# Feed-forward nets: hi and lo of x as one moving operand of 512 columns

## The chip, the cores and the metric

The kernel runs on one core of one Trainium2 chip. The metric is device time in microseconds (us) of one execution. The core has a matrix engine (TensorE, PE in the rows; its weight loads are shown as PEld), a vector engine (VectorE, DVE), an activation engine (ScalarE, ACT), a programmable engine (GpSimd, POOL) and a queue that issues transfers (SyncE, SP). Matrix products are written to PSUM, which here is used as eight banks of 128 x 512 float32. DVE and ACT read PSUM, GpSimd does not; SBUF is the memory that all engines share.

## The reference

x is 256 positions by 1024 channels. Four layers work on it, two of one kind of net and two of another, each a mixer (attention, a gated recurrence, or three attention branches) followed by a feed-forward net. The feed-forward nets are what the change touches:

```
def conv_ffn(h, w_in, conv_w, conv_b, w_out):            # nets 1 and 2, h = rms_norm(x)
    z = causal_dwconv(h @ w_in, conv_w, conv_b)          # w_in: 1024 x 5632
    u, g = jnp.split(z, 2, axis=-1)
    return (jax.nn.gelu(g) * u) @ w_out                  # w_out: 2816 x 1024

a = depthwise_conv(h @ w_ffn_gate, conv_w, conv_b)       # nets 3 and 4
x = x + (jax.nn.gelu(a) * (h @ w_ffn_up)) @ w_ffn_down
```

All is float32. The kernel keeps that precision with the faster float32r products: each operand is split into hi (rounded) and lo (the rest), and a product is hi*hi + hi*lo + lo*hi.

## The kernel before

All weights lie in DRAM as one stream of 240 chunks in the order of use. `_push` (L245) loads the next chunk of up to 128 x 2048 values on the SP queue into a tile st, ACT writes hi from it (L258) and DVE writes lo = st - hi (L259), each in two halves of 1024 columns. st, hi and lo have three buffers each, and `chunk` (L265) keeps two chunks ahead of the one in use.

`mm3` (L273 to L277) issues the three products of a split operand pair. In `tm_wide` (L289) the weights chunk is the moving operand, 512 columns at a time. In `fm_pair` (L299) and `fm_first` (L545) the weights chunk is what is loaded into the array and x, transposed (channels on partitions, 256 positions as columns), is the moving operand: for each block of 128 input channels k and each half e of the chunk there are a product of the hi weights with xh (L275), of the hi weights with xl (L276) and of the lo weights with xh (L277), each of 256 columns, all added up in the same 256 columns of a bank.

`norm` (L337) transposes x on PE into banks S and T and writes xh with ACT and xl with DVE, as two tiles. The factor 1/rms of each position is not put into xh and xl: `norm_rows` (L370) spreads it over the partitions as the tile rb, and `times_r` (L563) multiplies the finished products by it on DVE as it takes them out of PSUM (L568, L570).

`ffn` (L574) is one feed-forward net. It has 22 steps j. Each takes a chunk of 128 columns of u and 128 of g: `fm_first` does j = 0 and 1 in banks A, A and S, S, `fm` (L557) the others in one bank each, T and S in turn. Then `times_r`, the convolution `conv` (ACT at L537, then DVE per further tap at L540), gelu on ACT and the product with u on DVE (L604, L605 in nets 1 and 2, where u and g are both convolved; L615, L616 in nets 3 and 4, where g alone is), and `split` (ACT at L307, DVE at L308), which leaves hi and lo of the hidden block in hg tiles. From j = 5 on, after each odd j, one `tm_wide` multiplies the pair of blocks from two pairs earlier (LAG) with its rows of w_out into four banks A, A, A, O; the last two pairs follow after j = 21. Net 2 also runs `before_b` (L761) before its steps: positions, sines and other scalars of the next layers, with several tables loaded by ACT.

PSUM: one pool with tags A (3 banks), S (2), T (2), O (1). All tiles of one tag take its banks in turn, and a tile waits until the former one in its bank has been read.

The order within each engine's queue is set by the framework's planner, from the order in which the code names the instructions, their dependencies and its own costs; each engine then works through its queue in that order. An instruction that waits at the head of a queue holds up all that stands behind it. GpSimd has little to do before: some bias tables in attention (L863) and a few transfers.

Of the kernel before, what the change touches and what calls it, by code (L numbers as in the profile page):

```python
# [12 lines left out]
F32R = mybir.dt.float32r  # L13
I32 = mybir.dt.int32
AF = mybir.ActivationFunctionType
ALU = mybir.AluOpType
AX = mybir.AxisListType
PSUM = bass.MemoryType.PSUM

P = 128  # L20
S = 256
D = 1024
KD = D // P
# [174 lines left out]
class InOrder:  # L198


    def __init__(self, tc, engine):
        self.tc, self.engine = tc, engine
# [6 lines left out]
class Net:  # L209
    def __init__(self, ctx, tc, ap, out, shapes, vat, rat, upto=99):  # L210
        self.tc, self.nc, self.ap, self.out = tc, tc.nc, ap, out
        self.shapes, self.vat, self.rat, self.upto = shapes, vat, rat, upto
        self.sb = ctx.enter_context(tc.tile_pool(name="sb", bufs=1))
        self.ps = ctx.enter_context(tc.tile_pool(name="ps", bufs=1, space=PSUM))
        self.n = 0
        self.q, self.qpos, self.off = [], 0, 0
        self.ph = "s"
        self.vec_o, self.act_o = InOrder(tc, self.nc.vector), InOrder(tc, self.nc.scalar)
        self.pool_o, self.sync_o = InOrder(tc, self.nc.gpsimd), InOrder(tc, self.nc.sync)


    PS = {"A": 3, "S": 2, "T": 2, "O": 1}
    SB = {"st": 3, "hi": 3, "lo": 3, "o": 4, "hg": 8, "w6": 2, "w4": 6, "w2": 2, "qk": 2, "s": 4, "pT": 2, "bias": 2, "ty": 24, "at": 4}

    def t(self, shape, tag, dt=F32):
        self.n += 1
        pool = self.ps if tag in self.PS else self.sb
        return pool.tile(shape, dt, tag=tag, name=f"{tag}_{self.ph}_{self.n}", bufs=self.PS.get(tag) or self.SB.get(tag, 1))

    def bank(self, tag):  # L230
        return self.t([P, 512], tag)

    def wide_banks(self):
        return [[self.bank("A"), self.bank("A")], [self.bank("A"), self.bank("O")]]
# [97 lines left out]
    def update(self, t, n, banks):  # L332
        xs = self.x[:, t, n * 512:n * 512 + 512]
        if banks is not None:
            self.nc.vector.tensor_tensor(out=xs, in0=banks[t][n][:, :], in1=xs, op=ALU.add)

    def norm(self, gi, banks=None, update=None):  # L337


        nc = self.nc  # L340
        update = update or self.update
        xh = self.t([P, KD, S], "xh", F32R)
        xl = self.t([P, KD, S], "xl", F32R)
        ss = self.t([P, 2, 2], "ssx")
        for n in range(2):
            for t in range(2):
                update(t, n, banks)
            for kp in range(2):
                pt = self.bank("ST"[kp])
                for e in range(2):  # L350
                    k = 4 * n + 2 * kp + e
                    for t in range(2):
                        nc.tensor.transpose(pt[:, e * S + t * P:e * S + t * P + P], self.x[:, t, k * P:k * P + P], self.ident)
                for e in range(2):
                    k = 4 * n + 2 * kp + e
                    g = self.vec(f"gain{gi}", k)
                    z = pt[:, e * S:e * S + S]
                    nc.scalar.activation(xh[:, k, :], z, AF.Copy, scale=g)  # L358
                    nc.vector.scalar_tensor_tensor(xl[:, k, :], z, g, xh[:, k, :].bitcast(F32), op0=ALU.mult, op1=ALU.subtract)  # L359
        for n in range(2):  # L360
            for t in range(2):
                sq = self.t([P, 512], "w2")
                nc.scalar.activation(sq, self.x[:, t, n * 512:n * 512 + 512], AF.Square, scale=1.0 / 32, accum_out=ss[:, n, t:t + 1])
        m = self.t([P, 16], "ty")
        nc.vector.scalar_tensor_tensor(m[:, :2], ss[:, 0, :], EPS, ss[:, 1, :], op0=ALU.add, op1=ALU.add)
        self.r = self.t([P, 2], "r")
        self.rsqrt(m[:, :2], 2, self.r)
        return xh, xl

    def norm_rows(self):  # L370

        nc = self.nc
        dg = self.t([P, 2, P], "w2")
        pb = self.bank("T")
        for t in range(2):
            nc.scalar.activation(dg[:, t, :], self.ident, AF.Copy, scale=self.r[:, t:t + 1])
            nc.tensor.matmul(pb[:, t * P:t * P + P], self.ones, dg[:, t, :], start=True, stop=True)
        self.rb = self.t([P, S], "rb")
        nc.scalar.activation(self.rb, pb[:, :S], AF.Copy)
# [183 lines left out]
    def times_r(self, z, src):  # L563
# [7 lines left out]
                                    in1=self.rb[:, None, :].to_broadcast([P, 2, S]), op=ALU.mult)  # L571
        return z

    def ffn(self, gi, body, ahead=None):  # L574
        xh, xl = self.norm(gi, self.acc)
        first = self.fm_first(xh, xl)
        self.norm_rows()
        acc = None
        if ahead is not None:
            ahead()  # L580
        done = []
        for j in range(NF):
            if j % 2 == 0:
                hh, hl = self.t([P, 2, S], "hg", F32R), self.t([P, 2, S], "hg", F32R)
                done.append((hh, hl))
            z = self.times_r(self.t([P, 2, S], "s"), first[j] if j < 2 else self.fm(xh, xl, "TS"[j % 2]))
            m = body(j, z[:, 0, :], z[:, 1, :])
            self.split(hh[:, j % 2, :], hl[:, j % 2, :], m)
            if j % 2 and j > 2 * LAG:
                if acc is None:  # L590
                    acc = self.wide_banks()
                kk = j - 1 - 2 * LAG
                self.tm_wide(acc, *done[kk // 2], kk, False)
        for kk in range(NF - 2 * LAG, NF, 2):
            self.tm_wide(acc, *done[kk // 2], kk, kk == NF - 2)
        self.acc = acc

    def ffn_a(self, l, gi, ahead=None):
        nc = self.nc
# [512 lines left out]
    def hybrid(self, i, g0):  # L1112
        nc = self.nc
        xh, xl = self.norm(g0, self.acc, self.pending)
        if i:
            self.layer_scalars(i)
        c, kr, skr = self.mla_prep(i, xh, xl)
# [11 lines left out]
        for kind, b in MERGE:  # L1129
            if kind == "gate":  # L1130
                gates[b] = []
                for jp in range(4):
                    g = self.times_r(self.t([P, 2, S], "hg"), self.fm(xh, xl, "A")).rearrange("p e s -> p (e s)")
                    nc.scalar.activation(g, g, AF.Tanh, scale=0.5)
                    gates[b].append(g)
                continue
            if b == 2:
                mh, ml = self.t([P, KD, S], "xh", F32R), self.t([P, KD, S], "xl", F32R)
            for jp in range(4):
                if jp % 2 == 0:  # L1140
                    wh, wl = self.chunk(4, 512)
                bk = self.bank("A")
                self.fm_pair(bk, *outs[b], wh, wl, 4, (jp % 2) * 256)
                m = merged[jp // 2][:, jp % 2, :]
                g = gates[b][jp]
                if b == 0:
                    nc.vector.scalar_tensor_tensor(m, g, 1.0, bk, op0=ALU.add, op1=ALU.mult)
                else:
                    nc.vector.scalar_tensor_tensor(g, g, 1.0, bk, op0=ALU.add, op1=ALU.mult)
                    nc.vector.tensor_tensor(out=m, in0=m, in1=g, op=ALU.add)  # L1150
                if b == 2:
                    d = (slice(None), slice(2 * jp, 2 * jp + 2), slice(None))
                    m2 = m.rearrange("p (e s) -> p e s", e=2)
                    nc.scalar.activation(mh[d], m2, AF.Copy, scale=0.5)
                    nc.vector.scalar_tensor_tensor(ml[d], m2, 0.5, mh[d].bitcast(F32), op0=ALU.mult, op1=ALU.subtract)
# [12 lines left out]
        xh, xl = self.norm(g0 + 2, self.acc)  # L1168
# [4 lines left out]
        e = [self.t([P, D], "w4") for _ in range(2)]  # L1173
# [10 lines left out]
        for t in range(2):  # L1184
            for n in range(2):
                c = slice(n * 512, n * 512 + 512)
# [18 lines left out]
    def build(self):  # L1205
        nc = self.nc
        steps = [self.start, self.pool_attn, lambda: self.ffn_a(0, 1), lambda: self.rglru(2), lambda: self.ffn_a(1, 3, self.before_b),
                 lambda: self.hybrid(0, 4), lambda: self.hybrid(1, 7)]
        update = None
        for n, f in enumerate(steps[:self.upto + 1]):  # L1210
            self.ph = str(n)
            self.pending = update
            update = f()
        for n in range(2):
            for t in range(2):
                (update or self.update)(t, n, self.acc)
                c = slice(n * 512, n * 512 + 512)
                nc.sync.dma_start(self.out[t * P:t * P + P, c], self.x[:, t, c])


def _program(nc, tc, ap, out, shapes, vat, rat, upto=99):
# [14 lines left out]
```

## Time and profile before

| | |
|---|---|
| time, median of 3 runs (lowest to highest) | 1530.11 us (1529.07 to 1530.61) |
| time of the profiled execution | 1529.12 us |
| its span in the profile | 1527.4 us |
| busy PE, PEld | 1505.9 us (99%), 1354.4 us (89%) |
| busy DVE, ACT, POOL | 1136.1 us (74%), 940.3 us (62%), 53.7 us (4%) |
| instructions | 25319 |

The span goes from the first to the last instruction in the trace; 1.7 us of the execution lie around it. PE's records overlap each other (a product's record lasts longer than the distance to the next), so its busy share says only that it hardly ever paused; what a product costs is the distance from its start to the next one's start.

### The profile page before, as it was taken

To read this page: it belongs to the slowest core of one execution; us is meant where nothing else is said; L and a number is where in the kernel's file an instruction comes from. 1 tells how busy PE (TensorE), PEld (TensorE's weight loads), DVE (VectorE), ACT (ScalarE), POOL (GpSimd) and SP (SyncE) were. 2 spreads that over 40 slices of the span, in tenths; PEclk is the share of its full clock that TensorE was granted. 3 is DMA by queue.
4 is the path that set the end of the run, shared out by engine and by line. 5 is a ranking of instruction groups with operands and counts; after the bars stand their busy time and mean duration, and the time that the engine had idled before them with its cause. 6 is when DMAs were issued, how large, how long until landed. Compare 5 with 4: busy or idle time off the path is not lost.

```text
span 1527.4 us, 25319 instructions
## 1 busy us (share of the span) xinstructions
PE 1505.9 (99%) x10020; PEld 1354.4 (89%) x10020; DVE 1136.1 (74%) x2189; ACT 940.3 (62%) x1675; POOL 53.7 (4%) x45
## 2 busy tenths in 40 slices
PE   8999999999999999999999999999999999999998
PEld 6689999898999998898898999988888889999996
DVE  6559777789897777877677766678886767866666
ACT  6746555586675556676755655556777674654554
POOL 0200000000000000001110000000000110000000
PEclk9999999999999999999999999999999999999999
DMA  8445455434465554442444555444442435454551
GB/s 296 157 170 194 173 191 189 166 138 170 162 209 177 194 182 162 165 151 84 159 139 167 192 192 180 180 168 181 172 166 88 145 122 193 166 190 172 191 193 55
DMA packets 37878, 257.33 MB, mean 168 GB/s; under 512 B 4384, under 2 KB 4768, under 8 KB 8320
## 3 DMA queue, kind: packets, MB, share of 16 engines
q1 hardware_dynamic: 36864, 252.45, 46.2%
q0 software_dynamic: 896, 3.28, 0.6%
q8 instruction: 78, 1.28, 0.3%
q14 instruction: 40, 0.33, 0.1%
HBM read 254.66 MB, written 1.05 MB: 167 GB/s over the span
## 4 chain that ended last, share of the span: by engine, by line
PE 86%; DVE 7%; ACT 4%; issue 2%; DMA 0%; SPq 0%; ACTq 0%
PE A L276 13%; PE A L275 13%; PE A L277 13%; PE S L276 6%; PE S L277 6%; PE S L275 6%; PE T L277 6%; PE T L276 6%; PE T L275 5%; DVE lo L259 2%; PE O L275 2%; PE O L276 2%; PE O L277 2%; ACT hi L258 1%; PE T L817 1%
## 5 line engine op out<-in xcount | busy, mean ns | idle before, releaser
L259 DVE TENSOR_TENSOR lo<-st,hi 128x1024 fp32r<-128x1024 f32 (+2 forms) x480 | 572.0, 1208 | 163.6 <-ACT hi L258 160.7
L258 ACT ACTIVATE hi<-st 128x1024 fp32r<-128x1024 f32 (+2 forms) x480 | 489.0, 1042 | 243.5 <-PE T L276 110.0
L277 PE MATMUL S<-xh,lo 128*128 128x256 f32 x752 | 214.1, 285 | 0.0
L276 PE MATMUL S<-xl,hi 128*128 128x256 f32 x752 | 213.3, 284 | 0.0
L275 PE MATMUL S<-xh,hi 128*128 128x256 f32 x752 | 212.0, 282 | 0.0
L277 PE MATMUL T<-xh,lo 128*128 128x256 f32 x704 | 200.5, 285 | 0.0
L276 PE MATMUL T<-xl,hi 128*128 128x256 f32 x704 | 199.9, 284 | 0.0
L275 PE MATMUL T<-xh,hi 128*128 128x256 f32 x704 | 199.0, 283 | 0.0
L276 PE MATMUL A<-xl,hi 128*128 128x256 f32 x496 | 143.7, 290 | 1.2 <-DVE xl L359 1.1
L275 PE MATMUL A<-xh,hi 128*128 128x256 f32 x496 | 144.4, 292 | 0.0
L275 PEld LDWEIGHTS S<-xh,hi 128*128 128x128 f32 x752 | 142.7, 190 | 0.1
L277 PE MATMUL A<-xh,lo 128*128 128x256 f32 x496 | 142.3, 287 | 0.0
L277 PEld LDWEIGHTS S<-xh,lo 128*128 128x128 f32 x752 | 142.2, 189 | 0.1
L276 PEld LDWEIGHTS S<-xl,hi 128*128 128x128 f32 x752 | 141.7, 188 | 0.0
L275 PEld LDWEIGHTS T<-xh,hi 128*128 128x128 f32 x704 | 133.5, 190 | 1.6
L276 PEld LDWEIGHTS T<-xl,hi 128*128 128x128 f32 x704 | 132.6, 188 | 1.5
L277 PEld LDWEIGHTS T<-xh,lo 128*128 128x128 f32 x704 | 133.1, 189 | 0.1
L275 PE MATMUL A<-hi,xh 128*128 128x512 f32 (+2 forms) x336 | 129.4, 386 | 0.2 <-ACT xh L358 0.2
L276 PE MATMUL A<-lo,xh 128*128 128x512 f32 (+2 forms) x336 | 128.4, 383 | 0.3 <-DVE lo L259 0.3
L277 PE MATMUL A<-hi,xl 128*128 128x512 f32 (+2 forms) x336 | 127.9, 383 | 0.0
L276 PE MATMUL A<-lo,hg 128*128 128x512 f32 x294 | 116.2, 395 | 0.4 <-DVE lo L259 0.4
L275 PE MATMUL A<-hi,hg 128*128 128x512 f32 x294 | 116.2, 395 | 0.0
(343 smaller groups left out, 2966.1 us busy)
## 6 DMA issues: line engine op xcount, KB each, us to landing
st<-in_w_dram SPq DMA_DIRECT2D x230, 1024.0 KB, 4.8
st<-in_w_dram SPq DMA_DIRECT2D x4, 832.0 KB, 4.4
st<-in_w_dram SPq DMA_DIRECT2D x2, 768.0 KB, 5.1
x<-in_x_dram SPq DMA_DIRECT2D x2, 512.0 KB, 4.1
st<-in_w_dram SPq DMA_DIRECT2D x4, 256.0 KB, 6.7
st<-in_w_dram SPq DMA_DIRECT2D x2, 512.0 KB, 3.4
w<-in_gain_dram POOLq DMA_DIRECT2D x2, 512.0 KB, 3.6
out_dram<-x SPq DMA_DIRECT2D x4, 256.0 KB, 2.0
```

Source lines behind the costliest of these rows:

```text
L258: nc.scalar.activation(hi[:, c0:c1], st[:, c0:c1], AF.Copy)
L259: nc.vector.tensor_tensor(out=lo[:, c0:c1], in0=st[:, c0:c1], in1=hi[:, c0:c1].bitcast(F32), op=ALU.subtract)
L275: mm(out, ah, bh, start=start, stop=False)
L276: mm(out, ah, bl, start=False, stop=False)
L277: mm(out, al, bh, start=False, stop=stop)
L817: nc.tensor.transpose(pt[:, kb * S + t * P:kb * S + t * P + P], p[:, t * S + kb * P:t * S + kb * P + P], self.ident)
```

## The change

The feed-forward nets get xh and xl as one tile xx of 128 x 8 x 512: for each k, 256 columns of hi and behind them 256 of lo. The hi weights are multiplied with all 512 columns at once, and the lo weights with the first 256 (`mm2`). So the left half of a bank adds up hi*hi + lo*hi and the right half hi*lo, and a step needs two banks, one for each e. `join` adds the halves: ACT copies the right halves to SBUF (a tile y), DVE adds them to the left halves, and GpSimd multiplies the sum by rb. `times_r` is left to the other layers.

PSUM is now two pools: A and O as before, and a second half of four banks that is S, S, T, T outside of the feed-forward nets and D, D (two tiles of two banks) inside; it is closed and opened anew where a net begins and ends. In a net, `norm` and `norm_rows` take D tiles, `wide_first` does j = 0 and 1 in A, A, A, O, and `wide` does the others in D tiles. In the last mixer, the tiles mh and ml become halves of one xx tile.

```diff
-    PS = {"A": 3, "S": 2, "T": 2, "O": 1}
+    PS = {"A": 3, "S": 2, "T": 2, "O": 1, "D": 2}
...
+    def half_of_psum(self, name):
+        if self.ps2 is not None:
+            self.ps2_close()
+        cm = self.tc.tile_pool(name=f"ps_{name}_{self.n}", bufs=1, space=PSUM)
+        self.ps2 = cm.__enter__()
+        self.ps2_close = lambda: cm.__exit__(None, None, None)
+        self.doubles = name == "D"
...
-        xh = self.t([P, KD, S], "xh", F32R)
-        xl = self.t([P, KD, S], "xl", F32R)
+        self.xx = self.t([P, KD, 2 * S], "xx", F32R)
+        xh, xl = self.xx[:, :, :S], self.xx[:, :, S:]
...
+            both = self.t([P, 2, 512], "D") if self.doubles else None
...
-                pt = self.bank("ST"[kp])
+                pt = both[:, kp, :] if self.doubles else self.bank("ST"[kp])
...
+    def mm2(self, out, wh, wl, xx, start, stop):
+        mm = self.nc.tensor.matmul
+        mm(out, wh, xx, start=start, stop=False)
+        mm(out[:, :S], wl, xx[:, :S], start=False, stop=stop)
+
+    def wide_first(self):
+        xx = self.xx
+        w = [self.chunk(KD, 256) for _ in range(2)]
+        banks = self.wide_banks()
+        for k0 in (0, 4):
+            for j in range(2):
+                for e in range(2):
+                    for k in range(k0, k0 + 4):
+                        c = slice(e * P, e * P + P)
+                        self.mm2(banks[j][e], w[j][0][:, k, c], w[j][1][:, k, c], xx[:, k, :], k == 0, k == KD - 1)
+        return banks
+
+    def wide(self):
+        d = self.t([P, 2, 512], "D")
+        wh, wl = self.chunk(KD, 256)
+        for e in range(2):
+            for k in range(KD):
+                c = slice(e * P, e * P + P)
+                self.mm2(d[:, e, :], wh[:, k, c], wl[:, k, c], self.xx[:, k, :], k == 0, k == KD - 1)
+        return d
+
+    def join(self, z, src):
+        nc = self.nc
+        y = self.t([P, 2, S], "w2")
+        parts = [(z[:, e, :], y[:, e, :], src[e]) for e in range(2)] if isinstance(src, list) else [(z, y, src)]
+        for zz, yy, b in parts:
+            nc.scalar.activation(yy, b[..., S:], AF.Copy)
+            nc.vector.tensor_tensor(out=zz, in0=b[..., :S], in1=yy, op=ALU.add)
+        nc.gpsimd.tensor_tensor(out=z, in0=z, in1=self.rb[:, None, :].to_broadcast([P, 2, S]), op=ALU.mult)
+        return z
+
     def ffn(self, gi, body, ahead=None):
-        xh, xl = self.norm(gi, self.acc)
-        first = self.fm_first(xh, xl)
+        self.half_of_psum("D")
+        self.norm(gi, self.acc)
+        first = self.wide_first()
...
-            z = self.times_r(self.t([P, 2, S], "s"), first[j] if j < 2 else self.fm(xh, xl, "TS"[j % 2]))
+            z = self.join(self.t([P, 2, S], "s"), first[j] if j < 2 else self.wide())
...
         self.acc = acc
+        self.half_of_psum("ST")
```

## Rows read from the trace of the kernel before

**Rows 1.** From the page: busy time, and the chain that ended last.

```profile
PE 1505.9 (99%) x10020; PEld 1354.4 (89%) x10020; DVE 1136.1 (74%) x2189; ACT 940.3 (62%) x1675; POOL 53.7 (4%) x45
...
PE 86%; DVE 7%; ACT 4%; issue 2%; DMA 0%; SPq 0%; ACTq 0%
```

**Rows 2.** Busy time by stretch: length, PE, PEld, DVE, ACT, POOL, granted clock, DMA.

```profile
115.00:138.00 23.00, 23.00 (x196) 23.00 (x196) 22.51 (x44) 17.35 (x29) 0.00 (x0) 1.00 0.54 184
138.00:280.50 142.50, 142.50 (x987) 132.58 (x987) 110.17 (x170) 79.92 (x119) 0.00 (x0) 1.00 0.53 186
404.00:427.40 23.40, 23.40 (x197) 23.40 (x196) 23.36 (x78) 21.18 (x34) 3.59 (x2) 1.00 0.39 136
844.00:867.00 23.00, 23.00 (x194) 23.00 (x194) 20.83 (x34) 15.03 (x24) 0.00 (x0) 1.00 0.51 184
867.00:1009.00 142.00, 142.00 (x987) 132.39 (x986) 97.74 (x135) 72.64 (x101) 0.00 (x0) 1.00 0.52 186
```

**Rows 3.** Timeline of PE in net 1, start and length: first product per block.

```profile
194.88 0.28 PE L275 MATMUL T<-xh,hi 128*128 128x256 f32 x1
...
200.63 0.28 PE L275 MATMUL S<-xh,hi 128*128 128x256 f32 x1
...
206.40 0.40 PE L275 MATMUL A<-hi,hg 128*128 128x512 f32 x1
...
212.00 0.28 PE L275 MATMUL T<-xh,hi 128*128 128x256 f32 x1
```

**Rows 4.** Timeline of PE: four transposes of 128 columns to a row.

```profile
101.13 0.60 PE L353 MATMUL S<-ident,x 128*128 128x128 f32 x4
101.56 0.60 PE L353 MATMUL T<-ident,x 128*128 128x128 f32 x4
```

**Rows 5.** Groups by line: shapes, count, busy us and mean ns, idle before.

```profile
L570 DVE TENSOR_TENSOR s<-T,rb 128x512 f32<-128x512 f32 x43 | 29.7, 691 | 66.1 <-PE T L277 66.1
...
L819 ACT ACTIVATE pT<-T 128x512 f32<-128x512 f32 x40 | 23.6, 590 | 4.4 <-PE T L817 4.1
```

**Rows 6.** What DVE waited for from 138 to 280.5 us: total, times, longest.

```profile
DVE s L570 <- PE T L277: 15.7, 8, 2.0
DVE lo L259 <- ACT hi L258: 8.5, 16, 0.8
DVE hg L308 <- ACT hg L307: 3.9, 8, 0.5
DVE qk L605 <- ACT qk L604: 3.8, 7, 0.5
```

**Rows 7.** Two GpSimd operations, a cast beside them, and minimum, median, maximum of lines.

```profile
705.11 3.62 POOL L863 TENSOR_SCALAR bias<-dist 128x512 f32<-128x512 f32 x2 [294.55 <-DVE at L877]
...
706.16 1.22 DVE L259 TENSOR_TENSOR lo<-st,hi 128x1024 fp32r<-128x1024 f32 x1
...
L1039 DVE TENSOR_SCALAR ty<-at,neglam x8: 206/358/645, 708.0 to 1192.5; 128x2 f32<-128x2 f32 x8
...
L863 POOL TENSOR_SCALAR bias<-distw x16: 1479/1490/1793, 719.6 to 1237.1; 128x512 f32<-128x512 f32 x16
```

**Rows 8.** Timeline of PE, DVE and ACT around the first `tm_wide` of net 2.

```profile
415.88 0.28 PE L275 MATMUL T<-xh,hi 128*128 128x256 f32 x1
...
421.16 0.68 DVE L570 TENSOR_TENSOR s<-S,rb 128x512 f32<-128x512 f32 x1
...
425.61 1.05 ACT L258 ACTIVATE hi<-st 128x1024 fp32r<-128x1024 f32 x1
...
427.64 1.22 DVE L259 TENSOR_TENSOR lo<-st,hi 128x1024 fp32r<-128x1024 f32 x1
...
428.92 0.50 PE L276 MATMUL A<-lo,hg 128*128 128x512 f32 x1 [0.42 <-DVE lo L259]
```

**Rows 9.** Timeline of DVE and PE at the end of net 1.

```profile
282.91 0.42 DVE L308 TENSOR_TENSOR hg<-qk,hg 128x256 fp32r<-128x256 f32 x1
...
286.08 0.40 PE L275 MATMUL A<-hi,hg 128*128 128x512 f32 x1
```

More of the change, by code (lines that the diff above doesn't have):

```diff
@@ L214, in __init__ @@
         self.ps = ctx.enter_context(tc.tile_pool(name="ps", bufs=1, space=PSUM))
+        self.ps2, self.ps2_close = None, None
         self.n = 0
@@ L226, in t @@
         self.n += 1
-        pool = self.ps if tag in self.PS else self.sb
+        pool = self.sb if tag not in self.PS else self.ps if tag in "AO" else self.ps2
         return pool.tile(shape, dt, tag=tag, name=f"{tag}_{self.ph}_{self.n}", bufs=self.PS.get(tag) or self.SB.get(tag, 1))
@@ L373, in norm_rows @@
         dg = self.t([P, 2, P], "w2")
-        pb = self.bank("T")
+        pb = self.bank("D" if self.doubles else "T")
         for t in range(2):
@@ L1137, in hybrid @@
             if b == 2:
-                mh, ml = self.t([P, KD, S], "xh", F32R), self.t([P, KD, S], "xl", F32R)
+                mm = self.t([P, KD, 2 * S], "xx", F32R)
+                mh, ml = mm[:, :, :S], mm[:, :, S:]
             for jp in range(4):
@@ L1209, in build @@
         update = None
+        self.half_of_psum("ST")
         for n, f in enumerate(steps[:self.upto + 1]):
@@ L1218, in build @@
                 nc.sync.dma_start(self.out[t * P:t * P + P, c], self.x[:, t, c])
+        self.ps2_close()
 def _program(nc, tc, ap, out, shapes, vat, rat, upto=99):
```

## The prediction

> **What bounds the kernel now.** I read the page first: PE is busy 99% of the span, and 86% of the chain that ended last is PE [rows 1]. A busy share of overlapping records proves little, so the next view is busy time by stretch, over the four feed-forward nets: PE has no idle time in them, at a granted clock of 1.00, the 2.4 GHz level [rows 2]. In the steady part of nets 1 and 2 DVE is at 110.17 of 142.50 us (77%) and ACT at 79.92 (56%); in nets 3 and 4, which convolve g alone, DVE is at 97.74 of 142.00. But in the heads of the nets (j = 2 to 5, before the first `tm_wide`) DVE is at 22.51 of 23.00 us in net 1, 23.36 of 23.40 in net 2, where ACT is at 21.18 too, and 20.83 of 23.00 in net 3. So PE is the bound, and in two heads the others have nothing to spare.
>
> The timeline of PE gives the prices [rows 3]. The 48 products of a step take 200.63 - 194.88 = 5.75 us and the next 48 take 5.77, so 120 ns per 256 columns. The 24 products of a `tm_wide` take 212.00 - 206.40 = 5.60 us, 233.3 ns per 512 columns. A pair of steps with its `tm_wide` lasts 17.12 us.
>
> **What the change does, part by part.**
>
> *Products.* Per k and e, three of 256 columns (3 x 120 = 360 ns) become one of 512 and one of 256. Columns stay the same, 768; one issue and one weight load go. At the prices above the two cost 233.3 + 120 = 353.3 ns, 6.7 ns less. There are 4 nets x 22 steps x 2 halves x 8 k = 1408 of them: -9.4 us. This alternation is not in the trace. One bound: 512 columns cost as much as two times 256, gain 0; a loss I exclude, as nothing is streamed in addition. The other: a product beside a long one costs only what a 128-column transpose does, (101.56 - 101.13) / 4 = 108 ns [rows 4], so 341 ns and -26 us. I take -9.4, which uses prices of the same stretch. A pair of steps then lasts 32 x 0.3533 + 5.60 = 16.91 us.
>
> The Trainium skill (TensorE: Matmul & The Clock Gate, Back-to-back issue gap) gives a warm isolated product N/2.4 + 2.5 ns. An estimate from that page: 215.8 and 109.2 ns, so 2.5 ns saved per triple, 3.5 us in all. The rows, 233 and 120 ns, are longer than the rule, and the part that doesn't grow with the columns is larger in them, which speaks for the larger gain.
>
> *DVE.* The multiplication out of PSUM, 691 ns [rows 5], becomes an addition of the same shape with one operand from PSUM: 0.
>
> *ACT.* One copy of 128 x 512 out of PSUM per step; the nearest row is 590 ns [rows 5]. Per pair ACT goes from 79.92 / 142.5 x 17.12 = 9.6 to 10.8 of 16.9 us. It hides behind PE in the steady part.
>
> *GpSimd.* One product of 128 x 512 per step on an engine that does nothing else there. The trace has only one-input operations of that size: 1.49 us alone, and the two at 705.11 took 3.62 together, so one was stretched by 0.64 while a DVE cast ran [rows 7]. Between 1.49 us and twice that plus the stretch, 3.6; I take 2.2. It adds latency, not load. What it takes from DVE is between nothing (the cast at 706.16 ran beside it in 1.22 us, as did the one at 427.64 without [rows 8]) and 0.44 us (a small TENSOR_SCALAR, 645 ns against 206, [rows 7]); I take 0.2 per step. DVE per pair: 110.17 / 142.5 x 17.12 = 13.24, then 13.6 of 16.9. Its waits for ACT, 8.5 + 3.9 + 3.8 = 16.2 us in 8.3 pairs [rows 6], make 1.95 more: 15.6. It still fits, with 1.3 to spare; in nets 3 and 4 with far more.
>
> *Latency.* From the end of a step's products to hg, the way grows by copy, product and their hand-overs, about 0.6 + 2.2 + 0.2 = 3 us. Between steps the LAG of two pairs covers it. At the end of net 1 the last split starts at 282.91 and ends at 283.33, and `tm_wide` of that pair starts at 286.08 [rows 9]: a reserve of 2.75, so some 0.3 us late; 0.6 for nets 1 and 2. In 3 and 4 two taps less are on the way: 0.
>
> *Double banks.* A step may now be issued only when the step two before has been joined, where there were four banks of S and T. A D tile has one step (5.65 us) for its join in the heads, and one step and a `tm_wide` later. In net 2 the step that ends at 415.88 is taken out only from 421.16 to 421.84, 5.96 us later [rows 8]: this head is where depth runs out, and the copy comes on top.
>
> *Head of net 2.* ACT's queue holds the table loads of `before_b`, and the cast of the first `tm_wide` chunk (425.61, then DVE at 427.64) is already late: PE waits 0.42 us for it at 428.92 [rows 8]. Before that cast ACT gets copies of four steps, two of them in halves: about 5 x 0.6 = 3 us more in a stretch with 2.2 us idle, minus the 0.4 us by which PE itself comes earlier. I put the stall at +3.1 us (0 to 6). In net 1 ACT is at 17.35 of 23.00, DVE is full but gets only five times 0.2 us: 0.3.
>
> *Start of the nets.* The first product needs xl as well as xh, some 0.1 us per net. In return joining needn't wait for rb. 0.1 in all. The reopened pools wait for tiles that were read long before: 0. Weight stream, transfers and the other layers: unchanged, 0.
>
> *Sum.* -9.4 + 0.6 + 3.1 + 0.3 + 0.1 = -5.3 us, made against the profiled execution of 1529.12 us (span 1527.4 and 1.7 around it). This lies 1.0 us under the median of 1530.11; from the median, 1524.8. I predict 1525.
>
> **Rivals.** About 0.2%, 3.1 us, is what a measurement of this kernel can tell from no change.
>
> *The gain is used up at heads and tails.* The same gain, but the head of net 2 costs 5 us, that of net 1 one, and each of the four tails 0.5: -9.4 + 8 = -1.4, some 1529. For it: the head of net 2 is full on both engines, and the depth of banks there is short by the numbers of rows 8. Against it: 5 us is nearly two steps' reserve, and casts run two chunks ahead. A smaller gain of the product pair, as by the rule above, ends in the same place.
>
> *DVE becomes the bound in nets 1 and 2 (slower).* The queues work in a fixed order. If the convolution on ACT stands waiting for the GpSimd product, and DVE's taps behind it, the time that DVE stands still comes off its reserve. By rows 2, 3 and 6 the reserve is 16.91 - 13.24 - 1.95 = 1.7 us per pair, 0.85 per step: from there on it decides. At 1.49 us per step, the length of one GpSimd operation, a pair is 1.3 us too long: 9 pairs x 2 nets = 23 us, and the two heads, which have no reserve, some 5 steps x 1.0 us each, another 10. With -9.4: +24, about 1554; at 1.1 us per step 9 + 6 - 9.4 = +6, 1536. For it: the DVE share of 77% and the longer chain. Against it: DVE waits 15.7 us for PE, 1.9 per pair [rows 6] and has casts to put in between, and the casts in rows 7 were not slowed.
>
> The Trainium skill (SBUF — State Buffer, Who interferes with whom) says that a VectorE instruction with two SBUF inputs and a GpSimd one that reads SBUF exclude each other: whichever comes second is held fully. All casts and taps here are of that form. By that rule DVE would lose the whole of a GpSimd product wherever it came second, which is this rival. The trace shows the cast unhurt and GpSimd stretched, so it agrees for the case in which DVE comes first; of the other it shows only the 0.44 us.
>
> *A larger gain.* The weight loads weigh more than the columns say, and a pair of products costs near its lower bound of 341 ns: half of the way there is -18 us, with the heads 1516. For it: PEld is busy 89% [rows 1]. Against it: nearly twice the columns take nearly twice the time in rows 3.
>
> **How the numbers follow.** Forecast (1520 to 1527): 0.42. Larger gain (under 1520): 0.08. Used up at heads and tails (1527 to 1533): 0.25. DVE bound (over 1533): 0.25, half of it beyond 1548. So faster 0.50, same 0.25, slower 0.25. The likeliest case's own range is 1520 to 1527. The range for 8 in 10 is 1514 to 1550; it leaves out some 3% below and about 10% above.
>
> **What would show it.** In the steady part of net 1, a step of 32 products in about 5.65 us, a pair with `tm_wide` in about 16.9; GpSimd products near 2.2 us; DVE under 85% there; PE waiting a few us in the head of net 2 for a cast or a D tile. Wrong in the gain: a step of 5.75 us, or 5.4. Wrong in the costs: pauses of PE in each pair of nets 1 and 2, DVE waiting for ACT's convolution and casts late, which makes it slower.

## The result, and the profile after

| | before | with the change |
|---|---|---|
| time, median (lowest to highest), same chip | 1529.8 us (1529.07 to 1530.61) | 1546.55 us (1545.82 to 1547.9) |
| ratio, 95% interval | | 1.0113 [1.0101, 1.0125] |
| span of the profiled execution | 1527.4 us | 1545.1 us |

The change makes the kernel 1.1% slower, 16.8 us. The forecast was 1525, faster.

From the page of the changed kernel: busy time, the chain by engine, and three groups (line, engine, operation, count | busy, mean ns | idle before it and the releaser).

```profile
PE 1504.4 (97%) x8612; PEld 1284.5 (83%) x8612; DVE 1170.5 (76%) x2189; ACT 978.7 (63%) x1771; POOL 226.6 (15%) x133
PE 66%; DVE 17%; ACT 9%; issue 4%; POOL 3%; DMA 0%; SPq 0%; POOLq 0%; ACTq 0%; DVEq 0%
L621 POOL TENSOR_TENSOR s<-s,rb 128x512 f32<-128x512 f32 x88 | 173.1, 1969 | 698.5 <-DVE s L620 484.6
L548 ACT ACTIVATE pT<-s,vec 128x256 f32<-128x256 f32 x71 | 40.5, 597 | 112.9 <-POOL s L621 111.1
L548 ACT ACTIVATE qk<-s,vec 128x256 f32<-128x256 f32 x71 | 40.4, 597 | 81.5 <-POOL s L621 81.5
```

Against [rows 1], PE's share of the chain fell from 86% to 66%, and DVE, ACT and GpSimd came into it. ACT's convolution (L548) now waits 192.6 us for the GpSimd product. That alone proves nothing, since idle time of an engine that isn't the bound is free; so first the places where PE lost time.

PE's timeline in the steady part of net 3: two steps and a `tm_wide`.

```profile
949.40 0.40 PE L588 MATMUL D<-xx,hi 128*128 128x512 f32 x1
955.00 0.40 PE L588 MATMUL D<-xx,hi 128*128 128x512 f32 x1
960.62 0.39 PE L285 MATMUL A<-hi,hg 128*128 128x512 f32 x1
966.22 0.40 PE L588 MATMUL D<-xx,hi 128*128 128x512 f32 x1
```

A step takes 5.61 us where [rows 3] had 5.76, a `tm_wide` 5.60 as before, a pair 16.82. So 16 products of 512 and 16 of 256 columns cost 350.6 ns per two, against 360 for three: 9.4 ns less, 13.2 us in the 1408 of them. PE gained more than forecast. Measured on PE's starts in both profiled executions, section by section, and with the products' gain taken out, the rest was lost here (head: steps 2 to 5; steady part: from the first `tm_wide` to the end of step 21; tail: the last three `tm_wide`):

| where | change in length | products' part | cost |
|---|---|---|---|
| norm and first two steps, 4 nets (14.07 us became 15.64 each) | +6.3 | -1.2 | 7.5 |
| head and steady part of net 2 | +4.05 | -3.0 | 7.05 |
| head, steady part and tail of net 1 | -1.3 | -3.0 | 1.7 |
| heads and steady parts of nets 3 and 4 | -5.0 | -6.0 | 1.0 |
| tails of nets 3 and 4 (16.81 us became 22.51 and 23.69) | +12.6 | 0 | 12.6 |

The sum is 29.9 - 13.2 = +16.7 us. The first mixer was another 1.3 us longer in that execution; that is not the change's (last section).

The tail of net 3, on DVE, GpSimd, ACT and PE: the GpSimd product of step 19, then the last steps, j = 20 and 21.

```profile
1003.39 2.21 POOL L621 TENSOR_TENSOR s<-s,rb 128x512 f32<-128x512 f32 x1 [5.41 <-DVE s L620]
1010.84 0.58 ACT L619 ACTIVATE w<-D 128x512 f32<-128x512 f32 x1
1012.51 0.69 DVE L620 TENSOR_TENSOR s<-D,w 128x512 f32<-128x512 f32 x1
1013.28 2.21 POOL L621 TENSOR_TENSOR s<-s,rb 128x512 f32<-128x512 f32 x1 [7.68 <-DVE s L620]
1015.52 0.60 ACT L548 ACTIVATE pT<-s,vec 128x256 f32<-128x256 f32 x1 [3.15 <-POOL s L621]
1017.25 0.42 ACT L667 ACTIVATE pT<-pT 128x256 f32<-128x256 f32 x1 [1.13 <-DVE pT L553]
1018.52 0.40 ACT L317 ACTIVATE hg<-pT 128x256 fp32r<-128x256 f32 x1
1018.83 0.58 ACT L619 ACTIVATE w<-D 128x512 f32<-128x512 f32 x1
1020.89 2.21 POOL L621 TENSOR_TENSOR s<-s,rb 128x512 f32<-128x512 f32 x1 [5.41 <-DVE s L620]
1027.40 0.42 DVE L318 TENSOR_TENSOR hg<-qk,hg 128x256 fp32r<-128x256 f32 x1
```
```profile
1010.96 0.28 PE L589 MATMUL D<-xx,lo 128*128 128x256 f32 x1
1026.58 0.50 PE L285 MATMUL A<-hi,hg 128*128 128x512 f32 x1 [3.45 <-ACT hg L317]
```

Read it as a ring. The copy of step 20 is followed by add, GpSimd product, convolution, gelu and split, with the casts of weight chunks that the queues hold between them, and only then does ACT come to the copy of step 21: the products of 21 ended at 1011.1, and their copy waited until 1018.83 behind work of step 20 that was itself waiting. One turn of two steps lasts 17.50 us (the product starts at 1003.39 and again, two steps on, at 1020.89), PE's pair 16.82. So the join falls behind by 0.68 us per pair. An early and a late place of the same lag:

```profile
910.04 0.28 PE L589 MATMUL D<-xx,lo 128*128 128x256 f32 x1
...
913.84 0.58 ACT L619 ACTIVATE w<-D 128x512 f32<-128x512 f32 x1
```

The copy comes 3.80 us after the last product of its step here, 7.87 six pairs later, and between them it grows by 0.67 to 0.69 each time. Nothing shows while the LAG of two pairs covers it; PE runs without a pause until the tail, and pays there.

In net 1, whose body is longer, the same chain turned in 16.16 us:

```profile
216.71 1.29 POOL L621 TENSOR_TENSOR s<-s,rb 128x512 f32<-128x512 f32 x1 [4.80 <-DVE s L620]
...
232.87 1.30 POOL L621 TENSOR_TENSOR s<-s,rb 128x512 f32<-128x512 f32 x1 [4.80 <-DVE s L620]
```

There every other copy stands ahead of a split in ACT's queue (copy at 214.91, split of the step before at 216.34), and the lag, 8.63 us at most, shrinks by about 0.66 us per pair. So more work in a step doesn't by itself make the turn longer; the experiments test the order and the length of the chain.

### The profile page after: what moved, and what is told of

Same layout as the page of the kernel before. It is cut to its first block, busy times and chain, and to the rows that moved or that the text cites. A ratio compares the mean times of both kernels' runs of the same rounds, so it can differ in the third digit from the quotient of the medians.

```text
span 1545.1 us, 22736 instructions
## 1 busy us (share of the span) xinstructions
PE 1504.4 (97%) x8612; PEld 1284.5 (83%) x8612; DVE 1170.5 (76%) x2189; ACT 978.7 (63%) x1771; POOL 226.6 (15%) x133
## 4 chain that ended last, share of the span: by engine, by line
PE 66%; DVE 17%; ACT 9%; issue 4%; POOL 3%; DMA 0%; SPq 0%; POOLq 0%; ACTq 0%; DVEq 0%
PE D L588 11%; PE A L286 11%; PE A L287 11%; PE A L285 10%; DVE lo L269 7%; PE D L589 6%; ACT hi L268 3%; POOL s L621 3%; DVE pT L551 2%; DVE hg L318 1%; PE O L286 1%; PE O L287 1%; PE O L285 1%; DVE qk L551 1%; PE A L588 1%
## 5 line engine op out<-in xcount | busy, mean ns | idle before, releaser
L588 PE MATMUL D<-xx,hi 128*128 128x512 f32 x1280 | 452.8, 395 | 2.7 <-DVE s L620 2.7
L589 PE MATMUL D<-xx,lo 128*128 128x256 f32 x1280 | 362.2, 283 | 2.2 <-DVE lo L269 2.0
L588 PEld LDWEIGHTS D<-xx,hi 128*128 128x128 f32 x1280 | 241.1, 188 | 59.1 <-DVE s L620 2.5
L621 POOL TENSOR_TENSOR s<-s,rb 128x512 f32<-128x512 f32 x88 | 173.1, 1969 | 698.5 <-DVE s L620 484.6
L589 PEld LDWEIGHTS D<-xx,lo 128*128 128x128 f32 x1280 | 241.4, 189 | 4.5 <-DVE lo L269 3.1
L285 PE MATMUL A<-hi,xx 128*128 128x512 f32 (+2 forms) x336 | 129.1, 385 | 0.2 <-ACT xx L369 0.2
L286 PE MATMUL A<-lo,xx 128*128 128x512 f32 (+2 forms) x336 | 128.0, 382 | 0.4 <-DVE lo L269 0.4
L287 PE MATMUL A<-hi,xx 128*128 128x512 f32 (+2 forms) x336 | 127.7, 382 | 0.0
L286 PE MATMUL A<-xx,hi 128*128 128x256 f32 x432 | 125.4, 290 | 1.1 <-DVE xx L370 1.1
L285 PE MATMUL A<-xx,hi 128*128 128x256 f32 x432 | 125.7, 292 | 0.0
L287 PE MATMUL A<-xx,lo 128*128 128x256 f32 x432 | 124.4, 288 | 0.0
L548 ACT ACTIVATE pT<-s,vec 128x256 f32<-128x256 f32 x71 | 40.5, 597 | 112.9 <-POOL s L621 111.1
L548 ACT ACTIVATE qk<-s,vec 128x256 f32<-128x256 f32 x71 | 40.4, 597 | 81.5 <-POOL s L621 81.5
L286 PEld LDWEIGHTS A<-xx,hi 128*128 128x128 f32 x432 | 81.6, 189 | 6.3 <-issue 4.6
L285 PEld LDWEIGHTS A<-xx,hi 128*128 128x128 f32 x432 | 81.8, 190 | 1.7 <-issue 1.3
```

The lines of the kernel that those rows point to most:

```text
L285: mm(out, ah, bh, start=start, stop=False)
L286: mm(out, ah, bl, start=False, stop=False)
L287: mm(out, al, bh, start=False, stop=stop)
L548: nc.scalar.activation(c, src, AF.Identity, scale=w(i0), bias=self.vec(bname, j))
L588: mm(out, wh, xx, start=start, stop=False)
L589: mm(out[:, :S], wl, xx[:, :S], start=False, stop=stop)
```

## Experiments

**The ring, or the work itself.** Theory 1: the order in ACT's queue makes copy to split a ring of 17.5 us. Theory 2: two D tiles are too few. Theory 3: GpSimd slows DVE.

```diff
-        nc.gpsimd.tensor_tensor(out=z, in0=z, in1=self.rb[...], op=ALU.mult)
+        nc.vector.tensor_tensor(out=z, in0=z, in1=self.rb[...], op=ALU.mult)
```

> The product with rb goes from GpSimd to DVE (join: copy on ACT, add and multiply on DVE). Kernel with the change: 1546.55 us. Theory 1 (in nets 3 and 4 the way copy, add, GpSimd product, convolution, gelu, split, next copy is one ring through fixed queues, 17.5 us per pair of steps against 16.8 of PE; the copies fall behind by 0.67 us per pair and the two tails pay 12.6 us): the ring gets about 1.8 us per step shorter, the lag no longer grows, tails back at 16.8 us, 1534 (1531 to 1539). Theory 2 (two D tiles are too few): a shorter join frees them sooner, also some 1534. Theory 3 (GpSimd slows DVE down): the 513 ns of a tap go back to 480, same 1534. If DVE is at its limit in nets 1 and 2, the 0.6 us more per step show there as waits of PE: 1540 to 1550.

Measured 1529.86 us, ratio to before 1.0004 [0.9994, 1.0013]; 16.7 less than the change and 1.1 us under the expected range. Tails 16.80 us in all nets, the copies of net 3 never later than 1.47 us. All three theories say this of the tails, so it doesn't separate them. The expectation left out net 1, net 2 and the heads of nets 3 and 4, which together came out 4.4 us shorter than in the change; within net 2 the head got 3.1 us longer and the steady part 5.3 us shorter.

```diff
-        y = self.t([P, 2, S], "w2")
-        ... (copy, add, product)
...
+        nc.vector.tensor_tensor(out=z, in0=src[:, :, :S], in1=self.rb[...], op=ALU.mult)
```

> Products and banks as in the change, but the join is left out: one DVE multiplication of the left halves by rb, as before the change (this leaves out the hi x lo partial sums). It shows what PE's part costs alone. Theory 1 (the join's chain is what the tails and the head of net 2 pay for): tails 16.8 us, head of net 2 as before, 1546.5 - 12.6 - 4 - 0.5 = 1529.5 (1528 to 1532), that is the products' gain of some 9 us used up by norm (6.3) and first mixer (1.3) . Theory 2 (two D tiles are too few even so): tails stay above 18 us, 1535 to 1546.

Measured 1524.46 us, 0.9972 [0.996, 0.9983]: 5 us less than expected. Tails 16.80: two D tiles are enough for PE if the join is short. The miss is that the join had cost more than I put down: without it net 2 is 6.7 us shorter than in the change (4 expected), net 1 1.3 (0.5 expected), and the heads of nets 3 and 4 0.9 together (none expected); the first mixer, too, was 1.2 us shorter in this execution. Of the heads that of net 2 alone still pays (+1.1 us over the pace of its products).

```diff
...
             z = self.join(self.t([P, 2, S], "s"), first[j] if j < 2 else self.wide())
-            m = body(j, z[:, 0, :], z[:, 1, :])
-            self.split(hh[:, j % 2, :], hl[:, j % 2, :], m)
+            late.append((j, z, hh, hl))
+            if j:
+                finish(*late.pop(0))        # body and split of step j-1
...
```

> The code names the join of step j ahead of the convolution, gelu and split of step j-1, so that in ACT's queue the copy of j+1 stands ahead of the split of j; same operations on the same engines. Theory 1 (ring through ACT's queue order): the ring no longer holds gelu, product with u and split, the copies stay within 4 us of the end of their products, tails of nets 3 and 4 at 16.8 us, 1534 (1532 to 1538). Theory 3 (DVE is slowed by GpSimd): same work at the same time, 1546. Theory 2 (two D tiles): the copy comes no later than now, so no gain where PE doesn't wait for D: 1544 to 1547.

Measured 1539.85 us, 1.0069 [1.0054, 1.0084], 1.9 us over its range. Nets 3 and 4 did what theory 1 says: tails 16.81 and 16.80 us, the copies after 1.2 to 3.7 us with no growth, with all of the GpSimd work in place. Theories 2 and 3 fall for these tails. But in nets 1 and 2, with their longer bodies, the copies now came 5 to 8 us late to the end and the last pair with them (tails 6.8 and 5.1 us longer than before the change). Against the change net 1 lost 5.6 us by it, and net 2 only 0.8, as its head and steady part had become 4.3 us shorter. That is the miss in the main. So, in nets 3 and 4 alone (with the norm on S and T, as in the experiment on the start of the nets below):

```diff
...
-        self.ffn(gi, body)               # ffn_b
+        self.ffn(gi, body, behind=1)
```

> Norm on S and T, product on GpSimd in all nets, and in nets 3 and 4 alone the join of step j is named ahead of convolution, gelu and split of step j-1. Theory 1 (the ring through ACT's queue order is what the tails of nets 3 and 4 pay for): 1537.6 - 12.6 = 1525.0 (1523.5 to 1527). If GpSimd's work itself costs these tails: 1536 to 1538.

Measured 1523.16 us, 0.9962 [0.9948, 0.9976]: 14.4 us less than with that norm alone (1537.58), 0.3 under the range. Tails 16.80 us.

```diff
-        nc.gpsimd.tensor_tensor(out=z, in0=z, in1=self.rb[...], op=ALU.mult)
...
+            for e in (1, 0):             # nets 3 and 4
+                nc.gpsimd.tensor_tensor(out=z[:, e, :], in0=z[:, e, :], in1=rb, op=ALU.mult)
...
```

> Norm on S and T; in nets 3 and 4 the GpSimd product is issued as two of 128 x 256, the half that is convolved first, so that the convolution waits for half a product. Same columns and order otherwise. Theory 1: a ring of 17.5 us per pair of steps needs only 0.35 us less per step to fit into 16.8; half of 2.2 us is 1.1 less: no growth of the lag, tails 16.8 us, 1525.0 (1523.5 to 1527). Rival: a product of half the size costs nearly as much as a whole one (over 1.85 us): the lag goes on growing, 1532 to 1538. Theory that the total of GpSimd's work counts: 1537.6 or more.

Measured 1523.57 us, 0.9964 [0.9951, 0.9978], as expected. A half product took 1084 ns:

```profile
L629 POOL TENSOR_TENSOR s<-s,rb 128x256 f32<-128x256 f32 x88 | 93.8, 1084 | 375.5 <-DVE s L620 231.9 <-ACT rb L390 143.6
```

So GpSimd works longer in these nets (2.17 us a step, where whole products took 2.04), and yet the lag is gone (1.17 and 2.57 us from one pair to the next, to the end). It is the length of the ring, not the amount of work: settled for nets 3 and 4.

**The start of the nets.**

```diff
-        self.half_of_psum("D")
         self.norm(gi, self.acc)
+        self.half_of_psum("D")
```

> The norm ahead of each net takes the single banks S and T again, and the double banks are opened after it; all else as in the kernel with the change (1546.55 us). Theory: with D tiles and free A and O banks PE's queue mixes transposes and first products and waits 1.1 us for xx in between; norm and first two steps then take 15.64 us in place of 14.07, four times. Undone: 14.0 us each, 1546.5 - 6.3 = 1540 (1539 to 1542). Rival: the products wait for xl, which one moving operand needs at once: nothing changes, 1546 to 1547.

Measured 1537.58 us, 1.0054 [1.0039, 1.0069]: 9.0 less than the change, and 1.4 under the range, as norm and first two steps came down to 13.56 us and not to 14.0 only. From the first transpose to `norm_rows` PE's timeline has, with the change and with this edit:

```profile
102.44 0.38 PE L364 MATMUL D<-ident,x 128*128 128x128 f32 x2
...
117.72 0.61 PE L388 MATMUL D<-w,ones 128*128 128x128 f32 x4
```
```profile
101.22 0.60 PE L364 MATMUL S<-ident,x 128*128 128x128 f32 x4
...
114.42 0.61 PE L388 MATMUL D<-w,ones 128*128 128x128 f32 x4
```

15.28 and 13.20 us. That D tiles cost it is shown; my reason was PE's order (transposes behind products). Forced into the old order:

```diff
...
+                        if k == 0:
+                            self.after(one, self.tps)    # first products behind all 16 transposes
```

> The kernel with the change, norm on D tiles as there, but PE's order in norm is forced: all 16 transposes ahead of the first product, by an order-only dependency. Theory (the order is what costs: the last four transposes stand behind products, and the products of their channels then wait): norm and first two steps at 13.6 us in place of 15.64, 1546.5 - 8.2 = 1538.3 (1537 to 1540). Rival (the double banks cost: a tile of two banks comes free later): 15 us or more, 1545 to 1547.

Measured 1559.74 us, 1.0196 [1.0182, 1.021], the wrong way: neither the theory nor its rival. With the order forced the weight loads of the transposes (PEld, here in net 3) wait for DVE's reads:

```profile
PEld D L365 <- DVE xx L371: 3.5, 2, 1.9
```

The second half of a D tile is filled only when its first half has been read. The planner's mixed order had been hiding part of that: to `norm_rows` it took 15.28 us in net 1, the forced order 18.46. So, no reads between the transposes:

```diff
-            for kp in range(2):          # 4 transposes, their reads, 4 transposes, their reads
+            for kp in range(2):          # 8 transposes
+            ...
+            for kp in range(2):          # then their reads
```

> The kernel with the change; in norm the code names all eight transposes into a D tile ahead of the first read of it (before: four transposes, their reads, four transposes, their reads). Theory (a D tile is one object for the framework: the transposes into its second half wait until DVE has read its first half; forcing PE's order made that 3.4 us of waits per norm): the wait is gone and norm with first two steps takes 13.6 us in place of 15.64, 1546.5 - 8.2 = 1538.3 (1537 to 1540). Rival (the reads of two halves come too late for the first products in any case): 15 us, 1543 to 1546.

Measured 1546.14 us, 1.0114 [1.0097, 1.013]: nothing gained, the rival's side. The transposes no longer wait, but now the readers wait for each other (same net):

```profile
PEld A L589 <- DVE xx L371: 2.9, 2, 1.9
...
ACT xx L370 <- DVE xx L371: 1.1, 2, 1.0
```

ACT's reads of a tile, but for the first, now follow DVE's read of the block before; two of them show a wait (1.1 us), and PE's first products wait 2.9 us for DVE. On a D tile ACT and DVE take turns over four channel blocks, on a bank of S or T over two. What fits all three runs: for the order of its readers and writers a double bank counts as one tile, so two chains of eight reads replace four chains of four. The cost of the double banks is shown; this account of it rests on the waits.

**Net 2.** Here the scalars of the next layers (`before_b`) load ACT. First the two repairs together, then with the scalars moved:

```diff
-        if ahead is not None:
-            ahead()
...
+            if j == 8 and ahead is not None:
+                ahead()
```

> Both at once: the product with rb on DVE, and the norm on the single banks S and T. If the causes are separate, their gains add up: 1529.9 - 4 x 2.08 (norm and first two steps at 13.56 us in place of 15.64) - 1.4 (first mixer back at 101.2 us) = 1520.1 (1518.5 to 1522), with the head of net 2 still 2 us worse than before the change. If they share a cause: 1525 or more.

> As the one with the product on DVE and the norm on S and T, and the scalars and tables of the next layers (before_b) are named ahead of step 8 of net 2 instead of its head. Theory: the head of net 2 pays 5 us because ACT's tables and casts stand before the copies there and with two D tiles PE waits for the join; moved, head and steady part of net 2 come out as those of net 1 (0.3 and 2.3 us under before), 4.5 us less: 1515.6 (1514 to 1517.5). Rival: the load collides in the steady part just as well, or the next layer waits for it: 1519 to 1522.

Measured 1521.51 us, 0.9951 [0.9938, 0.9965], and 1515.88 us, 0.9913 [0.99, 0.9927]. Gains add up, and the second is faster than both kernels: 12.9 us, about the 13.2 of the products. The move alone, without the change:

> The kernel before the change, with the scalars and tables of the next layers named ahead of step 8 of net 2 (nothing else). In it the head of net 2 pays only some 0.4 us for them. Theory (the change's short double banks and its copies made that place dear): no change, 1528.8 (within 1 us); then the 1515.9 of the kernel with both is owed to the change's products, not to this move. Rival: the move is a gain of its own: 1524 or less.

Measured 1528.45 us, 0.9992 [0.9983, 1.0001]: no gain by itself that the runs can tell (in its profile net 2 is 0.95 us shorter). In the change it should then be worth 6 us:

> The kernel with the change, with the scalars and tables named ahead of step 8 of net 2 and nothing else. Theory: head and steady part of net 2 (4.1 us over before together) come out as those of net 1 (1.8 under): 1546.5 - 5.9 = 1540.6 (1539 to 1542.5). Rival (the join on GpSimd in net 2's head is late whatever ACT has besides): 1545 to 1547.

Measured 1546.13 us, 1.0108 [1.0094, 1.0122]: nothing. The head got 2.1 us shorter than in the change and the steady part 2.0 us longer; PE stood 5.0 us there. GpSimd's queue held two bias tables (L915) ahead of a product there. Taken away, alone and with the move:

```diff
-        self.nc.gpsimd.tensor_scalar(b, ..., -slope, None, op0=ALU.mult)
+        self.after(self.nc.gpsimd.tensor_scalar(b, ..., -slope, None, op0=ALU.mult), [self.product])
```

> The kernel with the change; GpSimd's two bias tables for the next layer (3.2 us at 409.7 us, in the head of net 2) are put behind the last product of net 2 by an order-only dependency. Theory A (these tables and their wait for the scalars of ACT hold GpSimd's queue, and the first products with them): the head and steady part of net 2, 4.1 us over before together, come out 1.8 us under, 1546.5 - 5.9 = 1540.6 (1539 to 1542.5). Theory B (ACT's queue with the tables of before_b and the copies is what is late): no change, 1545.5 to 1547. In between if both hold.

> The same, and the scalars and tables of the next layers are named ahead of step 8 of net 2. With the scalars moved alone the head was healed and PE then stood 5.1 us at 473.9 us, when GpSimd's bias tables (wait 5.9 us, run 4.0 us) held a product and a D tile with it. Theory A: without the tables in GpSimd's queue both are healed, 1546.1 - 5.9 = 1540.2 (1539 to 1542). Theory B (the later ACT load is what stops PE there): 1544 to 1547.

Measured 1544.97 us, 1.01 [1.0085, 1.0115], and 1545.22 us, 1.0103 [1.0088, 1.0118]: theory A has 0.9 to 1.6 us by the medians, 0.7 and 0.3 by PE's timeline of net 2, and not 6. ACT's timeline in the second:

```profile
469.21 1.28 ACT L206 ACT_TABLE_LOAD   x1
470.50 0.23 ACT L206 ACTIVATE trcos<-trcos 128x32 f32<-128x32 f32 x1
470.75 1.28 ACT L656 ACT_TABLE_LOAD   x1
472.05 0.42 ACT L656 ACTIVATE pT<-pT 128x256 f32<-128x256 f32 x1
472.48 1.28 ACT L206 ACT_TABLE_LOAD   x1
473.78 0.23 ACT L206 ACTIVATE trsin<-trsin 128x32 f32<-128x32 f32 x1
474.02 1.28 ACT L206 ACT_TABLE_LOAD   x1
475.32 0.29 ACT L206 ACTIVATE ty<-ty 128x1 f32<-128x1 f32 x2
475.52 0.40 ACT L317 ACTIVATE hg<-pT 128x256 fp32r<-128x256 f32 x1
475.83 0.57 ACT L619 ACTIVATE w<-D 128x512 f32<-128x512 f32 x1
```

Four table loads, 6.1 us from the first to the end of the last, stand ahead of a copy, and PE stood 4.2 us for the D tile. In the 1515.88 us kernel ACT has four loads in 6.6 us at the same place, but there the copies come 0.3 to 1.5 us after their products and reach 3.6; with the product on GpSimd they are 3 to 6 us late before the loads begin. So moving the scalars pays 5.6 us where the join is short and nothing where it is long. That it is the join's length that decides fits these rows; it was not tested alone, since the two kernels differ in the norm's banks as well.

## Why the prediction was wrong

It failed in the sum's small terms, not in the large one.

- *Products, -9.4.* Right in mechanism, mis-sized: 350.6 ns per two, not 353.3; -13.2. An estimate by the rule of the Trainium skill (TensorE: Matmul & The Clock Gate, Back-to-back issue gap) is 2.5 ns less per three; the rows gave 6.7, and 9.4 were measured.
- *Latency, "In 3 and 4 two taps less are on the way: 0".* The main failure: 12.6 us. I counted the way of one step and set it against the reserve at the end. A step's copy also stands in ACT's queue behind the step before, and a way that is in a ring with itself must be set against PE's pair: about 17.5 against 16.8. "Between steps the LAG of two pairs covers it" holds for a constant delay, not for one that grows.
- *Start of the nets, "0.1 in all".* 7.5 us. The line on double banks counted how many tiles there are, not that a tile is also the unit of waiting.
- *Head of net 2, +3.1 (0 to 6).* Right for the stretch it named: the head with its first `tm_wide` cost 3.3 us (the terms as written, 3 more, 2.2 idle and 0.4, don't give the 3.1). Another 3.8 us went in the two steps behind it, for which the sum had nothing. PE's pauses in the changed kernel:

```profile
421.11 0.50 PE L588 MATMUL D<-xx,hi 128*128 128x512 f32 x1 [2.17 <-DVE s L620]
435.02 0.50 PE L286 MATMUL A<-lo,hg 128*128 128x512 f32 x1 [1.25 <-DVE lo L269]
448.89 0.39 PE L589 MATMUL D<-xx,lo 128*128 128x256 f32 x1 [1.95 <-DVE lo L269]
```

  The first is for a D tile, the others for casts. The third lies in the two steps; from 439.5 to 454.5 us the granted clock was 0.89 in the mean. GpSimd's bias tables in front of the products, some 0.7 us, were not in the sum, though they are in GpSimd's queue.
- *Head and tail of net 1, +0.6.* 1.7 us: the head 0.3, as forecast, the tail 0.5, and 0.9 in the steady part.
- *GpSimd, 2.2 us.* 1.97 on average, 2.2 in the steady part of nets 3 and 4: right. *DVE, 0.2 us a step:* (1170.5 - 1136.1) / 88 = 0.39 on average, inside the bounds, but 0.5 and 0.6 in nets 1 and 2, above them; it was off the path.
- *Rivals.* The slower one named what happens (ACT's convolution waiting for the GpSimd product) and a range that held the time, but its place and its price were wrong: DVE was never the bound (92.75 of 132 us in net 3's steady part, 114.44 of 134 in net 1's), and nets 1 and 2 were not where most was lost. "Used up at heads and tails" had the places and half a microsecond for each tail.

## What to carry to other kernels

When an operation is put into a chain that repeats, follow the chain round until it meets itself in some engine's queue, and set that turn against the bound's period; a turn that is 4% too long is invisible for the whole loop and is paid at its end. Then reordering or shortening the ring repairs it (here naming a join earlier, or halving what the next link waits for), with no work removed. The same reordering made the nets with the longer body slower, so each loop needs its own check. Joining two buffers into one tile joins their waits too.

## What the runs showed of the hardware

GpSimd and DVE did hold each other here. The product runs 1.30 us when it comes first, and then it is DVE's split that is stretched, from 0.42 us to 1.51; behind a DVE cast it takes 2.14. Timelines of DVE and GpSimd in net 2 with the change:

```profile
535.91 1.22 DVE L269 TENSOR_TENSOR lo<-st,hi 128x1024 fp32r<-128x1024 f32 x1
536.14 2.14 POOL L621 TENSOR_TENSOR s<-s,rb 128x512 f32<-128x512 f32 x1 [8.58 <-DVE s L620]
...
543.09 1.30 POOL L621 TENSOR_TENSOR s<-s,rb 128x512 f32<-128x512 f32 x1 [4.80 <-DVE s L620]
543.15 1.51 DVE L318 TENSOR_TENSOR hg<-pT,hg 128x256 fp32r<-128x256 f32 x1 [0.21 <-ACT hg L317]
```

That is the case the trace of before left open: whichever comes second is held, as the Trainium skill says (SBUF — State Buffer, Who interferes with whom). So in net 1 the offload bought DVE nothing: it is busy 114.44 us of 134 with the product on GpSimd and 114.07 with it on DVE (windows: length, then busy PE, PEld, DVE, ACT, POOL, clock, DMA share, GB/s):

```profile
140.00:274.00 134.00, 133.78 (x699) 113.50 (x698) 114.44 (x165) 85.39 (x132) 28.95 (x16) 1.00 0.53 189
```
```profile
140.00:274.00 134.00, 134.00 (x703) 114.18 (x702) 114.07 (x179) 83.03 (x128) 0.00 (x0) 1.00 0.54 196
```

In net 3 it did bring something. There each product from 890.80 us to the tail starts 0.16 us behind the start of a DVE cast and is the one that is held, 2.20 us each time, and DVE is busy 92.75 us of 132, against 99.41 with the product on DVE. The cast beside the product at 1003.39 first:

```profile
1003.23 1.21 DVE L269 TENSOR_TENSOR lo<-st,hi 128x1024 fp32r<-128x1024 f32 x1
```

```profile
873.00:1005.00 132.00, 132.00 (x692) 112.40 (x691) 92.75 (x127) 72.02 (x109) 32.83 (x16) 1.00 0.52 184
```
```profile
873.00:1005.00 132.00, 132.00 (x691) 112.40 (x691) 99.41 (x143) 75.63 (x111) 0.00 (x0) 1.00 0.56 191
```

So the hold is a part of the ring: an estimate from these rows is that with products of 1.30 us a turn would last 17.50 - 2 x 0.9 = 15.7 us, less than PE's pair. No run took the hold away alone.

PE's pauses in the tails cost twice. Over the tail of net 3, in which PE stands 3.45 us, the granted clock is 0.94 in the mean, so part of it at the 1.2 GHz level; with the product on DVE PE doesn't pause, and it is 1.00, the 2.4 GHz level (windows of PE: length, busy, clock, DMA share, GB/s).

```profile
1003.00:1033.00 30.00, 26.06 (x118) 0.94 0.49 175
```
```profile
1003.00:1033.00 30.00, 30.00 (x144) 1.00 0.46 162
```

The first mixer's 1.3 us is the clock too, and not the change: the kernels with the join ahead in nets 3 and 4 and with half products have the same order of instructions there, and one was granted 1.00, the other 0.94 and was 1.3 us longer there. The kernel before with the scalars moved has the order of before in this stretch, and it too was granted 0.94 where before had 1.00, and came to its first transpose at 102.54 us, not 101.13. The rows are of the first two, in that order.

```profile
72.00:101.00 29.00, 27.67 (x121) 1.00 0.44 151
```
```profile
72.00:101.00 29.00, 27.70 (x115) 0.94 0.41 145
```
